# A hybrid DiT on one core: the gated-linear-attention chunk states by one scan per head over a chunk-innermost layout, in place of 38 vector steps

## The chip, the cores and the metric

The kernel runs on one core of one Trainium2 chip. The metric is the device time of one execution in microseconds; what stands below as before's time is the median of three runs.

## The reference

Two layers of a diffusion transformer on 1024 latent and 256 context tokens of width 1024. Layer 0 mixes the tokens with four DeltaNet heads and four gated-linear-attention (GLA) heads, both in two directions; layer 1 is attention; both end in a convolutional feed-forward. What is changed is the GLA heads' recurrence over chunks of 64 tokens:

```python
def _gla_chunked(q, k, v, log_a, s0):
    ...
    b = jnp.cumsum(log_a, axis=3)
    ...
    q_inter = q * jnp.exp(b)
    k_state = k * jnp.exp(b[..., -1:, :] - b)
    a_last = jnp.exp(b[..., -1, :])

    def step(S, xs):
        qd, kd, vc, al = xs
        o = qd @ S
        return S * al[..., :, None] + jnp.swapaxes(kd, -1, -2) @ vc, o

    xs = tuple(jnp.moveaxis(a, 2, 0) for a in (q_inter, k_state, v, a_last))
    S, o_inter = lax.scan(step, s0, xs)
```

There are 20 chunks, 4 of the context and 16 of the latents. The forward direction runs over the context and then the latents, the backward one over each of them from its end. A state is 64 x 128 per direction.

## The kernel before

The kernel is written as one long program; a scheduler then puts each engine's instructions into an order, and each engine runs its list in that order. All DMA transfers are issued from SyncE's queue. The pages below use these names of engines: PE is TensorE, DVE VectorE, ACT ScalarE, POOL GpSimd, SP SyncE.

The stage around the change lies at about 740 to 1040 us. In it four kinds of work are interleaved. `gla_prep(h)` does a GLA head, in the order of heads 0, 1, 3, 2. `gate_t` and `gate_p` project the output gates of all eight heads (tile `pj` on TensorE, 72 matrix products a head, `gt` on ScalarE and VectorE). `dn_run` runs the chunk steps of the last DeltaNet head (`dn_step`: `p`, `r`, `vn`, `sn`, `kd`, `q_`, `o_dn`). `merge` normalises a finished head (`o_g` or `o_d`, `msq`, `mss`, `pmt`) and writes it out for the output projection that follows (`m_scr`, `mt`).

`gla_prep` keeps both directions at once on the partitions: 0 to 63 are the forward one, 64 to 127 the backward one. It goes over the tokens in three groups (`GRP`: 512, 512 and 256). In each the gates' running sum is made by a scan inside the chunks (`g_b`, line 914), from it come the decays, among them `al`, the decay of a whole chunk, one column for each of the 20 chunks. The chunks' products `pgk` (line 953) are copied out of PSUM by ScalarE into `kv` (line 954), which holds 20 blocks of 128 columns. When a head's `kv` is filled, the 2 x 19 steps of the recurrence run on VectorE, each on 64 partitions and 128 columns, and write the state ahead of each chunk into `sst`; line 103 is the helper's line under which the trace shows them. At last the outputs `pgo` are summed in PSUM from the part inside the chunks (line 967, `att` by `v`) and the part from the states (line 970, `qi` by `sst`). One step and one output product read:

```python
            for n in range(19):
                stt(V, sst[0:64, n + 1], sst[0:64, n], al[0:64, n], kv[0:64, n], ALU.mult, ALU.add)
                i, j = SEQB[n], SEQB[n + 1]
                stt(V, sst[64:128, j], sst[64:128, i], al[64:128, i], kv[64:128, i], ALU.mult, ALU.add)
```

Two lines of an earlier stage matter for a price: `kk` turns round a tile inside each partition with ScalarE on partitions 0 to 63, and copies it straight on 64 to 103:

```python
            act(M[0:64], raw_[0:64].rearrange("p j i -> p i j"), AF.Copy, scale=-1.0)
            act(M[64:104], raw_[64:104], AF.Copy, scale=-1.0)
```

Of the kernel before, what the change touches and what calls it, by code (L numbers as in the profile page):

```python
# [9 lines left out]
F32 = mybir.dt.float32  # L10
F32R = mybir.dt.float32r
I32 = mybir.dt.int32
AF = mybir.ActivationFunctionType
ALU = mybir.AluOpType
# [56 lines left out]
def kernel(  # L71
# [4 lines left out]
    ffn_w_up, ffn_conv, ffn_w_down, final_norm, consts, rope, out, dbg=None, stop=None,  # L76
):
    nc = tc.nc
    V, S, G, T = nc.vector, nc.scalar, nc.gpsimd, nc.tensor

    def dma(o, i):
        o = o.bitcast(F32) if o.dtype == F32R else o
        i = i.bitcast(F32) if i.dtype == F32R else i
        nc.sync.dma_start(out=o, in_=i)
# [5 lines left out]
    def act(o, i, f, bias=0.0, scale=1.0):  # L90
        S.activation(out=o, in_=i, func=f, bias=bias, scale=scale)  # L91
# [10 lines left out]
    def stt(e, o, a, s, b, op0, op1):  # L102
        e.scalar_tensor_tensor(out=o, in0=a, scalar=s, in1=b, op0=op0, op1=op1)  # L103

    def pool(stack, name, bufs, psum=False, side=None):
        kw = {"space": PSUM} if psum else {}
        return stack.enter_context(tc.tile_pool(name=name, bufs=bufs, reuse_waits="tile", side=side, **kw))
# [152 lines left out]
    with ExitStack() as p0:  # L260
# [43 lines left out]
        for s_ in range(5):  # L304
            ci = 0 if s_ == 0 else (1 if s_ < 3 else 2)
            o = s_ * 256 - CHUNKS[ci][0]
            d = 1 if ci == 0 else 0
# [12 lines left out]
            t = tmp.tile([128, KD, 256], F32, tag="t", name="t", bufs=2)  # L320
# [47 lines left out]
    def projb(pj, w, sub, ci, n):  # L368
        ps = pj.tile([128, 512], F32, tag="pj", name="pj")
        for k in range(KD):  # L370
            hi, lo = w[k // 4]
            mm3(ps[:, 0:n], hi[:, k % 4, sub * 128:(sub + 1) * 128], lo[:, k % 4, sub * 128:(sub + 1) * 128],
                hhi[ci][:, k], hlo[ci][:, k], k == 0, k == KD - 1)
        return ps
# [100 lines left out]
    with loop:  # L475
# [15 lines left out]
        for ci, (t0, n) in enumerate(CHUNKS):  # L491
            ps = projb(pj, ws, 0, ci, n)
# [347 lines left out]
    with ExitStack() as tl:  # L840
# [4 lines left out]
        gb = pool(ti, "gb", 1)  # L845
# [41 lines left out]
                dma(m_scr[h8, :, t0:t0 + n], gt[:, 0:n])  # L887
            dump(f"m{h8}", m_scr[h8])

        SEQB = [3, 2, 1, 0] + list(range(19, 3, -1))  # L890
        GRP = ((0, 512), (512, 512), (1024, 256))

        def gla_prep(h):
            al = gb.tile([128, 20, 1], F32, tag="al", name="al", bufs=2)
            qi = gb.tile([128, NT], F32, tag="qi", name="qi", bufs=2)
            att = atts[h % 2]
            v = gb.tile([128, NB, 128], F32, tag="gv", name="gv")
            dma(v, gv_scr[h])
            kv = gb.tile([128, 20, 128], F32, tag="kv", name="kv")
            kv2 = kv.rearrange("p (b e) d -> p b e d", e=2)  # L900
            sst = gb.tile([128, 20, 128], F32, tag="sst", name="sst")
            for t0, n in GRP:
                c0, nc_, b0, nb = t0 // 64, n // 64, t0 // 128, n // 128
                ls = gs_.tile([128, 512], F32, tag="ls", name="g_ls", bufs=1)[:, 0:n]
# [2 lines left out]
                b = gs_.tile([128, 512], F32, tag="b", name="g_b")[:, 0:n]  # L907
                eb = gs_.tile([128, 512], F32, tag="eb", name="g_e")[:, 0:n]
                sm_ = gs_.tile([128, 4, 8, 1], F32, tag="gsm", name="gsm")[:, :, 0:nc_]
# [15 lines left out]
                tt(V, sm_[:, 2], sm_[:, 0], sm_[:, 1], ALU.subtract)  # L925
                act(sm_[:, 2], sm_[:, 2], AF.Exp, scale=1.0 / 16)
                act(sm_[:, 3], sm_[:, 1], AF.Exp, scale=1.0 / 16)
                act(al[:, c0:c0 + nc_], sm_[:, 0], AF.Exp, scale=1.0 / 16)
                stt(V, b, q, 0.125, b, ALU.mult, ALU.mult)
                tt(G, eb, k, eb, ALU.mult)  # L930
                tt(V, qi[:, t0:t0 + n].rearrange("p (c t) -> p c t", t=64), b3,
# [3 lines left out]
                for d in range(2):  # L935
                    pa_ = pm.tile([128, 4, 128], F32, tag="pm", name="pga")
                    for i in range(nb):
                        sl = slice(i * 128, (i + 1) * 128)
# [6 lines left out]
                ps = pm.tile([128, 4, 128], F32, tag="pm", name="pgt")  # L945
# [3 lines left out]
                for e in range(2):  # L949
                    ps = pm.tile([128, 4, 128], F32, tag="pm", name="pgk")  # L950
                    pe_ = slice(e * 64, (e + 1) * 64)
                    for i in range(nb):
                        T.matmul(ps[:, i], lhsT=kst[pe_, i], rhs=v[pe_, b0 + i], start=True, stop=True)
                    S.copy(out=kv2[:, b0:b0 + nb, e], in_=ps[:, 0:nb])
            G.memset(sst[0:64, 0], 0.0)
            G.memset(sst[64:128, SEQB[0]], 0.0)
            for n in range(19):
                stt(V, sst[0:64, n + 1], sst[0:64, n], al[0:64, n], kv[0:64, n], ALU.mult, ALU.add)
                i, j = SEQB[n], SEQB[n + 1]
                stt(V, sst[64:128, j], sst[64:128, i], al[64:128, i], kv[64:128, i], ALU.mult, ALU.add)  # L960
            o = gm.tile([128, NB, 128], F32, tag="og", name="o_g", bufs=2)
            for b0 in range(0, NB, 4):
                nb = min(4, NB - b0)
                ps = pm.tile([128, 4, 128], F32, tag="pm", name="pgo")
# [13 lines left out]
        gate_t(0)  # L978
        dn_run(NB)
        o0 = gla_prep(0)  # L980
        o1 = gla_prep(1)
        gate_t(4)
        merge(4, o0)
        gate_t(5)
        merge(1)
        gate_t(6)
        merge(5, o1)
        o3 = gla_prep(3)
        gate_t(2)
        o2 = gla_prep(2)  # L990
# [251 lines left out]
    with ExitStack() as p0:  # L1242
# [4 lines left out]
        with ExitStack() as po:  # L1247
# [32 lines left out]
            for ci in (0, 1, 2):  # L1280
                t0, n = CHUNKS[ci]
                d = 1 if ci == 0 else 0
# [3 lines left out]
                for dt in range(KD):  # L1286
# [3 lines left out]
                    ps = pu.tile([128, 512], F32, tag="u", name="po")  # L1290
# [15 lines left out]
        with ExitStack() as pf:  # L1306
# [7 lines left out]
            step = ffn_ctx(fa, raw, hx)  # L1314
# [13 lines left out]
    with ExitStack() as pf:  # L1328
        p = Ffn()
# [7 lines left out]
    with ExitStack() as pq:  # L1337
# [130 lines left out]
        with ExitStack() as pat:  # L1468
# [8 lines left out]
            scale = 128 ** -0.5  # L1477
# [77 lines left out]
            for i in range(nq + LP + 1):  # L1555
                if i < nq:
                    P_[i] = scores(*its[i // 2], i % 2)
                m = i - LT
                if 0 <= m < nq:
                    T_[m // 2] = transp(P_.pop(m), T_.get(m // 2), m % 2)  # L1560
                m = i - LP
# [8 lines left out]
    with ExitStack() as pe:  # L1570
        ops = ffn_ops(pool(pe, "hE1", 1, side="right"))
        p = Ffn()
# [9 lines left out]
    with ExitStack() as pz:  # L1582
# [4 lines left out]
        for ci in (1, 2):  # L1587
            for b in range(4):
# [3 lines left out]
                for hf in range(2):  # L1592
                    ps = (pu, pd)[(hf if ci == 2 else 0)].tile([128, 512], F32, tag="ud"[(hf if ci == 2 else 0)], name="zt")
# [8 lines left out]
                for hf in range(2):  # L1602
                    sl = slice(hf * 512, (hf + 1) * 512)
# [37 lines left out]
```

## Time and profile before

| | |
|---|---|
| runs | 3491.35, 3484.76, 3500.26 us; median 3491.35 |
| profiled execution, its span | 3491.3 us, 49121 instructions |
| TensorE (PE) busy | 3180.2 us, 91% |
| VectorE (DVE) busy | 2499.8 us, 72% |
| GpSimd (POOL) busy | 1732.5 us, 50% |
| ScalarE (ACT) busy | 1375.7 us, 39% |
| mean granted TensorE clock | 0.954 of full speed |

Busy time is the time in which an engine has an instruction running. It is an average over stages that differ, so what a change in one stage does is read from the stretches of that stage. The granted clock is the share of TensorE's full speed that the chip gave it.

### The profile page before, as it was taken

How to read it: one execution, taken by the hardware profiler on the slowest of the kernel's cores; microseconds unless marked ns; L12 is line 12 of the kernel's file. 1: busy time of each engine (PE TensorE's matmuls, PEld its weight loads, DVE VectorE, ACT ScalarE, POOL GpSimd, SP SyncE). 2: the span in 40 equal slices, each digit the busy share in tenths (PEclk: the TensorE clock that was granted, in tenths of full speed). 3: DMA queues.
4: the chain of work that ended last, by engine and by line, in shares of the span. 5: the costliest groups of instructions: out<-in, count | busy, mean ns of one | idle time of the engine just before them, and what ended most of it. 6: DMA issues, size and time to landing. Idle time of an engine off the chain costs nothing.

```text
span 3491.3 us, 49121 instructions
## 1 busy us (share of the span) xinstructions
PE 3180.2 (91%) x17300; PEld 2678.4 (77%) x17300; DVE 2499.8 (72%) x4119; ACT 1375.7 (39%) x2968; POOL 1732.5 (50%) x1611
## 2 busy tenths in 40 slices
PE   7877988899978988899999998889999799999998
PEld 4766867787767888678888877878888678887877
DVE  5776466668848699776767777887657777767677
ACT  4423133644443455433333323236656433323333
POOL 2364464523335566555555653663333565555554
PEclk9988989999988999999999998999999899999999
DMA  5546455545487444211111211550110111111112
GB/s 187 149 126 167 126 146 146 152 154 171 154 255 213 126 142 136 85 52 58 49 58 48 59 58 60 172 150 28 36 56 29 37 49 43 52 58 49 58 48 74
DMA packets 446165, 350.25 MB, mean 100 GB/s; under 512 B 56756, under 2 KB 392862, under 8 KB 445150
## 3 DMA queue, kind: packets, MB, share of 16 engines
q1 hardware_dynamic: 445918, 347.10, 33.2%
q8 instruction: 137, 2.24, 0.3%
q14 instruction: 110, 0.90, 0.1%
HBM read 286.25 MB, written 60.76 MB: 99 GB/s over the span
## 4 chain that ended last, share of the span: by engine, by line
PE 55%; DVE 21%; DMA 10%; issue 5%; ACT 4%; POOL 4%; SPq 1%; DVEq 0%; ACTq 0%; POOLq 0%
PE fg L157 6%; PE fg L155 6%; PE fg L156 6%; DMA mw<-in_mod_w_dram 4%; PE fd L156 4%; PE fd L157 4%; PE fd L155 4%; DVE macc L103 3%; DVE st L94 2%; DVE ft L103 2%; PE apo L155 2%; PE apo L157 2%; PE apo L156 2%; PE apt L1519 2%; PE pj L155 2%
## 5 line engine op out<-in xcount | busy, mean ns | idle before, releaser
L103 DVE SCALAR_TENSOR_TENSOR xT<-fd,mod,xT 128x512 f32<-128x512 f32 (+1 forms) x480 | 311.0, 671 | 185.3 <-PE fd L157 185.0
L103 DVE SCALAR_TENSOR_TENSOR macc<-mw,sc,macc 128x256 f32<-128x256 f32 (+2 forms) x301 | 241.1, 837 | 73.2 <-DMA mw<-in_mod_w_dram 72.0
L155 PE MATMUL pj<-hhi,whi 128*128 128x512 f32 (+1 forms) x696 | 264.5, 380 | 23.0 <-ACT raw L510 14.8
L156 PE MATMUL fd<-gl,dh 128*128 128x512 f32 (+1 forms) x688 | 267.5, 389 | 7.3 <-DVE gl L94 7.2
L157 PE MATMUL fd<-gh,dl 128*128 128x512 f32 (+1 forms) x688 | 266.7, 388 | 0.0
L155 PE MATMUL fd<-gh,dh 128*128 128x512 f32 (+1 forms) x688 | 262.7, 392 | 1.4 <-ACT gh L1143 1.1
L156 PE MATMUL pj<-hlo,whi 128*128 128x512 f32 (+1 forms) x696 | 262.3, 377 | 0.3 <-DVE hlo L94 0.3
L157 PE MATMUL pj<-hhi,wlo 128*128 128x512 f32 (+1 forms) x696 | 261.7, 376 | 0.0
L94 DVE TENSOR_TENSOR st<-st 128x512 f32<-128x512 f32 x176 | 211.4, 1201 | 47.5 <-POOL s1l L94 34.1
L100 POOL TENSOR_SCALAR P<-P,rc 128x512 f32<-128x512 f32 (+1 forms) x192 | 116.6, 627 | 199.3 <-DVE rc L1505 58.5
L94 POOL TENSOR_TENSOR dl<-sd,dh 128x256 fp32r<-128x256 f32 x168 | 156.4, 946 | 108.6 <-ACT dh L160 108.6
L103 DVE SCALAR_TENSOR_TENSOR ft<-fraw,conv_f,ft 128x1024 f32<-128x1024 f32 (+1 forms) x132 | 169.9, 1287 | 30.1 <-ACT ft L91 29.2
L94 POOL TENSOR_TENSOR w0l<-st,w0h 128x1024 fp32r<-128x1024 f32 x44 | 107.1, 2434 | 145.1 <-ACT w0h L1088 130.6
L155 PEld LDWEIGHTS pj<-hhi,whi 128*128 128x128 f32 x696 | 139.6, 201 | 47.1 <-ACT raw L510 16.3
L94 POOL TENSOR_TENSOR wl<-st,wh 128x512 fp32r<-128x512 f32 x88 | 128.4, 1472 | 83.8 <-ACT wh L160 79.4
L94 POOL TENSOR_TENSOR p<-p,u 128x512 f32<-128x512 f32 (+1 forms) x45 | 94.2, 2093 | 150.6 <-DVE u L94 150.6
L156 PEld LDWEIGHTS fd<-gl,dh 128*128 128x128 f32 x688 | 129.9, 189 | 39.9 <-DVE gl L94 13.5
L155 PEld LDWEIGHTS fd<-gh,dh 128*128 128x128 f32 x688 | 128.1, 189 | 36.6 <-ACT gh L1143 11.3
L156 PEld LDWEIGHTS pj<-hlo,whi 128*128 128x128 f32 x696 | 139.7, 201 | 19.3 <-DVE hlo L94 0.7
L157 PEld LDWEIGHTS pj<-hhi,wlo 128*128 128x128 f32 x696 | 139.2, 200 | 18.8 <-issue 0.2
L157 PEld LDWEIGHTS fd<-gh,dl 128*128 128x128 f32 x688 | 129.9, 189 | 26.3
L156 PE MATMUL fg<-al,w0h 128*128 128x512 f32 (+1 forms) x360 | 141.3, 392 | 6.1 <-DVE al L94 6.1
(623 smaller groups left out, 10466.5 us busy)
## 6 DMA issues: line engine op xcount, KB each, us to landing
st<-in_ffn_w_up_dram SPq DMA_DIRECT2D x88, 512.0 KB
st<-in_ffn_w_up_dram SPq DMA_DIRECT2D x88, 256.0 KB
sd<-in_ffn_w_down_dram SPq DMA_DIRECT2D x176, 128.0 KB
sh<-sh_scr SPq DMA_DIRECT2D x80, 256.0 KB
mw<-in_mod_w_dram SPq DMA_DIRECT2D x128, 128.0 KB
wst<-in_rec_w_in_dram SPq DMA_DIRECT2D x56, 256.0 KB
st<-in_rec_w_out_dram SPq DMA_DIRECT2D x24, 512.0 KB
mw<-in_mod_w_dram SPq DMA_DIRECT2D x24, 512.0 KB
```

What stands on the lines that cost most here:

```text
L94: e.tensor_tensor(out=o, in0=a, in1=b, op=op)
L100: e.tensor_scalar(out=o, in0=a, scalar1=s1, scalar2=s2, op0=op0, op1=op1)
L103: e.scalar_tensor_tensor(out=o, in0=a, scalar=s, in1=b, op0=op0, op1=op1)
L155: T.matmul(ps, lhsT=wh, rhs=xh, start=first, stop=False)
L156: T.matmul(ps, lhsT=wh, rhs=xl, start=False, stop=False)
L157: T.matmul(ps, lhsT=wl, rhs=xh, start=False, stop=last)
L1519: T.transpose(pt_[:, b], P[:, (b0 + b) * 128:(b0 + b + 1) * 128], ident)
```

## The change

The 38 steps become one scan instruction of VectorE over all 128 x 20 columns of a head, both directions at once: in a row of 20 positions the state of a position is the state before it times `d0` plus `kv`. For that `kv` is laid out with the chunks innermost (128 columns of 20 chunks each, so that consecutive state columns of one chunk lie 20 floats, 80 bytes, apart), and shifted by one, with the backward direction turned round: `slots` says which chunk goes to which position. Position 0 is set to zero in `kv` (by GpSimd) and in `al` (by VectorE), so that a row starts anew. `al` is filled by 14 small ScalarE instructions a head in place of 3, `kv` by 14 copies out of PSUM in place of 6. `d0` is `al` repeated for the 128 columns, one ScalarE copy of 128 x 2560; it takes the buffer that `sst` takes after it. The scan works in place on `kv`. Then three ScalarE copies bring the states back into `sst` in the order in which the products read it, two of them backwards. No transfer and no matrix product changes.

```diff
--- before.py
+++ after.py
@@ -887,18 +887,34 @@
                 dma(m_scr[h8, :, t0:t0 + n], gt[:, 0:n])
             dump(f"m{h8}", m_scr[h8])
 
-        SEQB = [3, 2, 1, 0] + list(range(19, 3, -1))
+        def slots(first, n, e, d):
+
+
+            out_ = []
+            for i in range(n):
+                c = 2 * (first + i) + e
+                to = c + 1 if d == 0 else (4 - c if c < 4 else 24 - c)
+                if to == 20:
+                    continue
+                if out_ and out_[-1][0] + out_[-1][1] == i and to == out_[-1][2] + (2 - 4 * d) * out_[-1][1]:
+                    out_[-1][1] += 1
+                else:
+                    out_.append([i, 1, to])
+            step = 2 - 4 * d
+            ends = [t + step * (m - 1) + (1 if step > 0 else -1) for _, m, t in out_]
+            return [(i, m, slice(t, z if z >= 0 else None, step)) for (i, m, t), z in zip(out_, ends)]
+
         GRP = ((0, 512), (512, 512), (1024, 256))
 
         def gla_prep(h):
-            al = gb.tile([128, 20, 1], F32, tag="al", name="al", bufs=2)
+            al = gb.tile([128, 20], F32, tag="al", name="al", bufs=2)
+            V.memset(al[:, 0:1], 0.0)
             qi = gb.tile([128, NT], F32, tag="qi", name="qi", bufs=2)
             att = atts[h % 2]
             v = gb.tile([128, NB, 128], F32, tag="gv", name="gv")
             dma(v, gv_scr[h])
-            kv = gb.tile([128, 20, 128], F32, tag="kv", name="kv")
-            kv2 = kv.rearrange("p (b e) d -> p b e d", e=2)
-            sst = gb.tile([128, 20, 128], F32, tag="sst", name="sst")
+            kv = gb.tile([128, 128, 20], F32, tag="kv", name="kv")
+            G.memset(kv[:, :, 0:1], 0.0)
             for t0, n in GRP:
                 c0, nc_, b0, nb = t0 // 64, n // 64, t0 // 128, n // 128
                 ls = gs_.tile([128, 512], F32, tag="ls", name="g_ls", bufs=1)[:, 0:n]
@@ -925,7 +941,11 @@
                 tt(V, sm_[:, 2], sm_[:, 0], sm_[:, 1], ALU.subtract)
                 act(sm_[:, 2], sm_[:, 2], AF.Exp, scale=1.0 / 16)
                 act(sm_[:, 3], sm_[:, 1], AF.Exp, scale=1.0 / 16)
-                act(al[:, c0:c0 + nc_], sm_[:, 0], AF.Exp, scale=1.0 / 16)
+                for d in range(2):
+                    pd_ = slice(d * 64, (d + 1) * 64)
+                    for e in range(2):
+                        for i, m, sl in slots(b0, nb, e, d):
+                            act(al[pd_, sl], sm_[pd_, 0, 2 * i + e:2 * (i + m - 1) + e + 1:2, 0], AF.Exp, scale=1.0 / 16)
                 stt(V, b, q, 0.125, b, ALU.mult, ALU.mult)
                 tt(G, eb, k, eb, ALU.mult)
                 tt(V, qi[:, t0:t0 + n].rearrange("p (c t) -> p c t", t=64), b3,
@@ -951,13 +971,19 @@
                     pe_ = slice(e * 64, (e + 1) * 64)
                     for i in range(nb):
                         T.matmul(ps[:, i], lhsT=kst[pe_, i], rhs=v[pe_, b0 + i], start=True, stop=True)
-                    S.copy(out=kv2[:, b0:b0 + nb, e], in_=ps[:, 0:nb])
-            G.memset(sst[0:64, 0], 0.0)
-            G.memset(sst[64:128, SEQB[0]], 0.0)
-            for n in range(19):
-                stt(V, sst[0:64, n + 1], sst[0:64, n], al[0:64, n], kv[0:64, n], ALU.mult, ALU.add)
-                i, j = SEQB[n], SEQB[n + 1]
-                stt(V, sst[64:128, j], sst[64:128, i], al[64:128, i], kv[64:128, i], ALU.mult, ALU.add)
+                    for d in range(2):
+                        pd_ = slice(d * 64, (d + 1) * 64)
+                        for i, m, sl in slots(b0, nb, e, d):
+                            S.copy(out=kv[pd_, :, sl].rearrange("p d n -> p n d"), in_=ps[pd_, i:i + m])
+            d0 = gb.tile([128, 128, 20], F32, tag="sst", name="d0")
+            S.copy(out=d0, in_=al[:, None, :].to_broadcast([128, 128, 20]))
+            kvf = kv.rearrange("p d n -> p (d n)")
+            V.tensor_tensor_scan(kvf, d0.rearrange("p d n -> p (d n)"), kvf, 0.0, ALU.mult, ALU.add)
+            sst = gb.tile([128, 20, 128], F32, tag="sst", name="sst")
+            kvn = kv.rearrange("p d n -> p n d")
+            S.copy(out=sst[0:64], in_=kvn[0:64])
+            S.copy(out=sst[64:128, 0:4], in_=kvn[64:128, 3::-1])
+            S.copy(out=sst[64:128, 4:20], in_=kvn[64:128, 19:3:-1])
             o = gm.tile([128, NB, 128], F32, tag="og", name="o_g", bufs=2)
             for b0 in range(0, NB, 4):
                 nb = min(4, NB - b0)
```

What the program's order becomes, at two engines. First TensorE at the last head (head 2), from its last chunk products `pgk` on; the lines with `p` are the DeltaNet head's, `pmt` is another head's merge. Before:

```order
L953 MATMUL pgk<-gv,kst 128x128 x4
L967 MATMUL pgo<-gv,attb_6944 128x128
L970 MATMUL pgo<-sst,qi 64x128 x2
L967 MATMUL pgo<-gv,attb_6944 128x128
L970 MATMUL pgo<-sst,qi 64x128
L421 MATMUL p_7309<-vn,kd 128x128
L422 MATMUL p_7309<-vn,dd 128x128
L408 MATMUL p_7321<-sn,sh 128x128
L409 MATMUL p_7321<-sn,sh 128x128
L970 MATMUL pgo<-sst,qi 64x128
L967 MATMUL pgo<-gv,attb_6944 128x128 x2
```

and after, where the same lines of the code are 973 (`pgk`), 993 and 996 (`pgo`):

```order
L973 MATMUL pgk<-gv,kst 128x128 x4
L993 MATMUL pgo<-gv,attb_6944 128x128
L421 MATMUL p_7356<-vn,kd 128x128
L422 MATMUL p_7356<-vn,dd 128x128
L408 MATMUL p_7369<-sn,sh 128x128
L409 MATMUL p_7369<-sn,sh 128x128
L885 MATMUL pmt<-ident,o_g 128x128 x2
L993 MATMUL pgo<-gv,attb_6944 128x128 x2
L417 MATMUL p_7376<-r,dd 128x128
L996 MATMUL pgo<-sst,qi 64x128 x2
```

The first product that reads `sst` stood second behind `pgk`; seven small products of other kinds and two more of `pgo`'s inner part stand ahead of it now. At the end of head 0 some 60 products stand between, most of them gate projections.

Then ScalarE at the end of head 0 (`q_`, `vn` and `kd` are the DeltaNet head's, `gt` is the eviction of a gate projection, `whi` a part of a weight). Before:

```order
L954 COPY kv<-pgk 128x2x128
L91 ACTIVATE gsm<-gsm 128x8
L954 COPY kv<-pgk 128x2x128
L91 ACTIVATE g_e<-g_b 128x512
L91 ACTIVATE gsm<-gsm 128x8
L91 ACTIVATE g_b<-g_b 128x512
L91 ACTIVATE kd<-sh,ekc 128x128
L160 CAST whi<-wst 128x512
L91 ACTIVATE q__6335<-p_6330,eG 128x128
```

and after (977 fills `kv`, 984 to 986 are the copies into `sst`):

```order
L977 COPY kv<-pgk 64x2x128 x2
L977 COPY kv<-pgk 64x128
L977 COPY kv<-pgk 64x2x128
L91 ACTIVATE q__6335<-p_6330,eG 128x128
L160 CAST whi<-wst 128x512
L91 ACTIVATE gt<-pj 128x512
L419 COPY vn<-p_6337 128x128
L984 COPY sst<-kv 64x2560
L985 COPY sst<-kv 64x512
L986 COPY sst<-kv 64x2048
L91 ACTIVATE kd<-sh,ekc 128x128
```

Two copies have become four, and the three long copies, which need VectorE's scan, stand ahead of the next `kd`, `q_` and `gt` of ScalarE.

## Rows read from the trace of the kernel before

**Rows 1.** The page's part 1: busy us and share of the span.

```profile
PE 3180.2 (91%) x17300; PEld 2678.4 (77%) x17300; DVE 2499.8 (72%) x4119; ACT 1375.7 (39%) x2968; POOL 1732.5 (50%) x1611
```

**Rows 2.** Busy time by 20-us stretches: PE, PEld, DVE, ACT, POOL, clock, DMA share, GB/s.

```profile
780.00:800.00 20.00, 16.74 (x98) 12.54 (x98) 18.70 (x37) 7.38 (x22) 9.42 (x9) 1.00 0.33 95
800.00:820.00 20.00, 18.94 (x132) 15.25 (x132) 12.90 (x31) 11.94 (x58) 5.91 (x8) 1.00 0.58 179
820.00:840.00 20.00, 18.64 (x122) 15.54 (x122) 19.57 (x45) 6.76 (x18) 8.84 (x8) 1.00 0.45 140
840.00:860.00 20.00, 17.67 (x107) 13.50 (x107) 19.11 (x41) 6.13 (x21) 6.80 (x6) 0.91 0.58 189
860.00:880.00 20.00, 19.12 (x138) 16.18 (x137) 10.53 (x24) 11.94 (x55) 8.51 (x9) 1.00 0.68 215
880.00:900.00 20.00, 18.92 (x113) 14.99 (x112) 19.43 (x48) 7.67 (x22) 5.92 (x6) 1.00 0.60 178
900.00:920.00 20.00, 16.20 (x102) 13.24 (x101) 19.25 (x38) 5.59 (x17) 7.33 (x6) 0.83 0.36 113
920.00:940.00 20.00, 20.00 (x124) 15.41 (x122) 14.29 (x36) 11.75 (x57) 7.53 (x7) 1.00 0.57 181
...
980.00:1000.00 20.00, 11.47 (x58) 9.64 (x56) 9.16 (x24) 7.87 (x20) 8.14 (x7) 0.74 0.81 237
1000.00:1020.00 20.00, 10.04 (x46) 8.29 (x46) 4.61 (x11) 9.35 (x30) 9.41 (x5) 0.59 0.94 299
```

**Rows 3.** The same for `sst` alone: PE, PEld, DVE, POOL, clock, DMA share.

```profile
780.00:800.00 20.00, 2.18 (x16) 0.97 (x16) 10.76 (x18) 0.00 (x0) 1.00 0.33 95
...
820.00:840.00 20.00, 0.00 (x0) 0.00 (x0) 6.75 (x15) 0.00 (x0) 1.00 0.45 140
840.00:860.00 20.00, 3.78 (x24) 1.65 (x24) 9.99 (x23) 0.00 (x0) 0.91 0.58 189
...
880.00:900.00 20.00, 0.00 (x0) 0.00 (x0) 6.66 (x15) 0.00 (x0) 1.00 0.60 178
900.00:920.00 20.00, 1.76 (x16) 0.79 (x16) 10.20 (x18) 0.00 (x0) 0.83 0.36 113
```

**Rows 4.** Groups by line and form, 740 to 1030 us: count, busy, mean ns, idle.

```profile
L103 DVE SCALAR_TENSOR_TENSOR sst<-sst,al,kv 64x128 f32<-64x128 f32 x152 | 67.7, 445 | 7.0 <-ACT kv L954 3.3 <-POOL wlo L94 0.2
...
L954 ACT COPY kv<-pgk 128x512 f32<-128x512 f32 x16 | 9.0, 582 | 3.4 <-PE pgk L953 3.3
...
L914 DVE TENSOR_TENSOR_SCAN g_b<-reset,g_ls 128x512 f32<-128x512 f32 x6 | 7.2, 1203 | 0.0
...
L914 DVE TENSOR_TENSOR_SCAN g_b<-reset,g_ls 128x256 f32<-128x256 f32 x4 | 2.7, 679 | 0.0
L954 ACT COPY kv<-pgk 128x256 f32<-128x256 f32 x8 | 2.7, 376 | 1.3 <-PE pgk L953 1.3
```

**Rows 5.** ScalarE's groups by line and form over the whole span.

```profile
L91 ACT ACTIVATE M<-pp 64x1024 f32<-64x1024 f32 x4 | 8.2, 2058 | 14.8 <-DMA pp<-nd_scr 14.8
...
L91 ACT ACTIVATE rm_sq<-xT 128x2048 f32<-128x2048 f32 x4 | 7.5, 1911 | 7.5 <-DVE xT L103 7.5
...
L91 ACT ACTIVATE M<-pp 40x1024 f32<-40x1024 f32 x4 | 4.2, 1054 | 0.1
```

**Rows 6.** TensorE's timeline in gate projections: start, us, what.

```profile
812.60 0.40 PE L156 MATMUL pj<-hlo,whi 128*128 128x512 f32 x1
812.83 0.40 PE L157 MATMUL pj<-hhi,wlo 128*128 128x512 f32 x1
813.07 0.38 PE L421 MATMUL p<-vn,kd 128*128 128x128 f32 x2
813.29 0.39 PE L422 MATMUL p<-vn,dd 128*128 128x128 f32 x2
```

**Rows 7.** TensorE's timeline after the last head: first and fifth DeltaNet round.

```profile
976.54 0.38 PE L421 MATMUL p<-vn,kd 128*128 128x128 f32 x2
...
990.99 0.49 PE L421 MATMUL p<-vn,kd 128*128 128x128 f32 x2 [0.41 <-ACT vn L419]
```

## The prediction

> **What bounds the kernel now.** I began with the page's table of engines [rows 1]: TensorE is busy for 91% of the span, VectorE for 72%, ScalarE for 39%. Over the whole program TensorE is the bound, so the change can only gain where TensorE waits. The second view is therefore the table by 20-us stretches over the stage in which the recurrence runs [rows 2]. There VectorE alternates: in five stretches (780, 820, 840, 880 and 900) it is busy for 18.7 to 19.6 of 20 us, and in those TensorE is busy for 16.20 to 18.92 only, at a granted clock down to 0.91 and 0.83. In the three stretches between them in which a head ends (800, 860, 920) VectorE falls to 10.5–14.3, while ScalarE rises from about 6–7 to 11.8–11.9. From 980 to 1020 TensorE is down to 11.47 and 10.04, with the DMA engines 81% and 94% busy: that is the tail of the stage, not bound by VectorE.
>
> The third view takes the same stretches for the state tile `sst` alone [rows 3]: VectorE's 18 + 15 + 23 + 15 + 18 recurrence steps take 44.36 us of its 96.06 in the five saturated stretches. In the grouped lines [rows 4] all 152 steps cost 67.7 us, 445 ns each. So the operation that the change takes off VectorE is what saturates it there.
>
> **A. What VectorE's relief gives back.** In the five stretches TensorE is idle for 100 − 88.17 = 11.8 us, and its clock is short by 20 × 0.09 + 20 × 0.17 = 5.2 us' worth [rows 2]. VectorE would have at most 96.06 − 44.36 + 4 × 5.4 = 73.3 us to do there in place of 96.06 (5.4 is the scan, below), so it would no longer bind. The most it can give is 11.8 + 5.2 = 17.0 us; I take **−17**, which is generous, and half of it, −8.5, as the other end. TensorE's 17 us are all that this stage can give back: a gain above 0.5% (17.5 us; about what a measurement of this kernel can tell from no change) would need all of it and nothing lost.
>
> **B. The new serial wait at each head's end.** Before, a step needs only its own chunk's product, so most of the 38 steps run while later products are still made, and the first output product `pgo<-sst` can run once its chunk's state is there. After, nothing can start before the last chunk product of the head is in `kv`, and then come three things in a row, on three engines.
>
> The last group's copies of `kv` out of PSUM: four in the new order, split by direction, where two of 376 ns stood [rows 4]; a copy's time goes by its elements per partition, so 4 × 376 = 1.5 us.
> The scan over 2560 elements of a partition. The scans that the kernel has take 1203 ns for 512 and 679 for 256 [rows 4], 2.05 ns an element, so 679 + 2304 × 2.05 = 5.4 us. Its inputs lie in a row, as theirs do.
> The three ScalarE copies of 2560, 512 and 2048 elements that turn `kv` back into `sst`; they read with a stride of 80 bytes. The nearest strided read is `M<-pp` in `kk` (a 32x32 transpose inside each partition), which reads at 128 bytes over 64 partitions: 2058 ns for 1024 elements, against 1054 for the one behind it, over the other 40 partitions, that reads straight [rows 5]. Taking off some 0.17 us an instruction (what is left of 582 and 376 at 0.80 ns an element [rows 4]), that is 1.84 ns an element: 5120 × 1.84 + 3 × 0.17 = 9.9 us. At the straight price (1911 for 2048 [rows 5], 0.84 ns an element) it is 4.8. I take 9.9, because the only row with such a stride says so; that two copies also run backwards no row prices, and I give it nothing.
> With some 0.6 us for three hand-offs the wait is 1.5 + 5.4 + 9.9 + 0.6 = **17.4 us** (12.3 at the straight price).
>
> The Trainium skill, "Advanced Engine Details and Errata", section "SBUF Cachelines", says that SBUF works in lines of 16 bytes and that an access pattern needs at least two hits on a line to hide the access time. The trace agrees for reads, 2058 against 1054 ns [rows 5], and by that rule the copies would be dear, as I take them. It makes no exception for writes; what that would do is the third rival.
>
> What hides this wait is what TensorE has between the last `pgk` and the first `pgo<-sst` in its new order. For head 0 that is 27 projections of 512 columns, 24 of 256 and 9 small ones; the starts of 512-column ones lie 0.23 us apart, those of small ones 0.22 (two passes each) [rows 6], and 256 columns get half of 0.23, so 6.2 + 2.9 + 2.0 = 11.1 us. Heads 1 and 3 have 12.4 and 11.7 in the same way (27 + 24 + 15, 28 + 24 + 11). The last head, 2, has 7 small products: 1.5 us. TensorE so stands for 17.4 − 11.1 = 6.3, then 5.0, 5.7 and 15.9 us: **+32.9**. At the straight price it stands for 1.2, 0, 0.6 and 10.8: +12.6.
>
> **C. ScalarE fuller, and others queued behind it.** ScalarE runs in order. The broadcast copy `d0` (2560 elements, straight: 2.3 us) and the three copies add 12.2 us a head. The stretches after a head's end have 11.9 us of ScalarE's time taken already [rows 2]: 24.1 of 20, 4.1 too much, 12.3 for the three. Its neighbours (6.8, 6.1, 7.7, 5.6) can take part of it. While the copies run, the evictions of the gate projections (`gt<-pj`), the DeltaNet's `vn`, `kd` and `q_` stand behind them. I take a third, **+4**, between 0 and 12.3. The small copies of `al` (14 for 3), the two memsets and VectorE's `al` column cost nothing in the sum: they stand among the work of the earlier groups, where ScalarE and GpSimd are busy for less than half of most stretches [rows 2]. If uncovered, the last group's four of `al`, each below the 376 ns of a 256-column copy, would add up to 1.5 us a head.
>
> **D. The tail.** The DeltaNet rounds left over after the last head end the stage: after the last `pgo` before has seven, the first at 976.54 and the fifth at 990.99, 3.6 us apart [rows 7]. In the new order five stand behind the last `pgo<-sst`, two within the wait. So 2 × 3.6 = **−7.2**.
>
> Sum: −17 + 32.9 + 4 − 7.2 = +12.7. The profiled execution's span is 3491.3, the median of the runs 3491.35, so nothing has to be added: **3504 us**.
>
> **The rivals.**
> *Strided reads at the straight price.* For it: an 80-byte stride is less than the row's 128. Against it: both rows are of the same engine and line, and both patterns touch each 4 bytes far from the last. B is 12.6: −17 + 12.6 + 4 − 7.2 = −7.6, **3484**.
> *ScalarE becomes the bound* (the other side). The new `kv` copies write at 80 bytes; no row has ScalarE writing with a stride. If a write costs as a strided read does, 11.7 us of `kv` copies in the stage [rows 4] become about 23, 2.9 more a head, of which some 1 us is in the last group's, on the path: 4 us. The stretch after a head is then 27.0 of 20 in place of 24.1, 3 × 2.9 = 8.7 more that the neighbours no longer take. +12.7 + 4 + 8.7 = +25.4: **3517**. It decides where ScalarE is over some 17 of 20 us in two stretches running. For it: a projection's eviction is one of those that queue, and TensorE has just so many PSUM buffers to write. Against: ScalarE is at 39% over all. The skill's rule quoted above speaks for it.
> *The last head's wait is hidden by the tail.* From 980 the DMA engines are 81 and 94% busy [rows 2], and what ends the stage may be transfers that go on during the wait. Then the last 15.9 and D fall away: −17 + 17.0 + 4 = +4, **3495**. Against it: the DeltaNet rounds wait for ScalarE's `vn`, not for a transfer, and `vn` stands behind the copies.
>
> **How the numbers follow.** The forecast, 3504 (its own range 3495 to 3514), has 0.40: 0.28 of it within 0.5% (3474 to 3509), 0.12 slower. Strided reads straight: 0.22 (0.05 faster, 0.17 same): faster needs the last head hidden too (B 1.8), C at nothing, and TensorE's idle time at 800 and 860 back as well (1.06 + 0.88 [rows 2]), −17 + 1.8 − 1.9 = −17.1. ScalarE the bound: 0.24 (0.22 slower, 0.02 same). Hidden last head: 0.14 (0.03 faster, 0.11 same). Together 0.08 faster, 0.58 same, 0.34 slower. The range goes from that −17.1, 3474, to the upper ends of the terms, −8.5 + 32.9 + 4 + 12.3 − 7.2 = +33.5: 3525.
>
> **What the new profile would show.** The scan at 5.4 us and the copies at 4.9, 1.1 and 3.9 (straight: 2.3, 0.6, 1.9); the last-group `kv` copies at 0.2 to 0.4 each, or twice that (third rival). VectorE below 16 of 20 in every stretch of 780 to 960. TensorE idle before `pgo<-sst` for some 5 to 6 us with ScalarE's `sst` copies as releaser, thrice, and about 16 us before the last head's. If these waits are under 2 us, the forecast is too high; if TensorE waits for `gt<-pj` instead, too low. It would also be wrong if the relief on VectorE gave TensorE nothing, since its waits in those stretches were for something else.

## The result and the profile after

The changed kernel took 3536.84 us in the median (3534.07 to 3550.45) against 3488.06 us for the kernel before in the same comparison: ratio 1.0139, 95% interval 1.0118 to 1.016, so slower by some 48 us. The forecast was 3504 with a range up to 3525. The profiled execution has a span of 3532.5 us, 41.2 more than before's.

The page's first part, after; beside [rows 1] ScalarE has 94 us more and VectorE 29 less:

```profile
PE 3193.1 (90%) x17300; PEld 2689.1 (76%) x17300; DVE 2470.7 (70%) x3975; ACT 1469.5 (42%) x3060; POOL 1743.6 (49%) x1607
```

The groups of lines by form in the stage (740 to 1080 us): count, then busy us and mean ns, then the idle time before. They answer to [rows 4, 5]:

```profile
L977 ACT COPY kv<-pgk 64x512 f32<-64x512 f32 x24 | 29.2, 1215 | 1.2 <-PE pgk L973 1.0
L984 ACT COPY sst<-kv 64x2560 f32<-64x2560 f32 x4 | 22.1, 5524 | 17.0 <-DVE kv L981 17.0
L981 DVE TENSOR_TENSOR_SCAN kv<-d,kv 128x2560 f32<-128x2560 f32 x4 | 22.0, 5512 | 4.4 <-ACT kv L977 4.4
...
L986 ACT COPY sst<-kv 64x2048 f32<-64x2048 f32 x4 | 17.8, 4446 | 0.0
...
L977 ACT COPY kv<-pgk 64x256 f32<-64x256 f32 x24 | 15.7, 694 | 0.8 <-PE pgk L973 0.6
...
L979 ACT COPY d<-al 128x2560 f32<-128x2560 f32 x4 | 9.3, 2330 | 0.1
...
L985 ACT COPY sst<-kv 64x512 f32<-64x512 f32 x4 | 5.0, 1251 | 0.0
...
L977 ACT COPY kv<-pgk 64x128 f32<-64x128 f32 x8 | 3.6, 450 | 0.1
```

The scan and `d0` cost what was forecast (5.4 and 2.3 us). The copies into `sst` cost 11.2 us a head in place of 9.9. The `kv` copies cost 48.5 us in place of before's 11.7: a 512-element one takes 1215 ns where it took 582, and there are 56 in place of 24.

The table by 20-us stretches, after (columns as in [rows 2]):

```profile
780.00:800.00 20.00, 18.17 (x116) 15.27 (x116) 14.58 (x21) 14.39 (x30) 12.42 (x8) 1.00 0.41 125
800.00:820.00 20.00, 16.76 (x88) 12.10 (x89) 3.54 (x9) 15.73 (x22) 3.69 (x5) 0.83 0.30 92
820.00:840.00 20.00, 19.64 (x134) 16.95 (x135) 16.70 (x34) 17.87 (x58) 11.39 (x9) 1.00 0.50 158
...
860.00:880.00 20.00, 13.72 (x74) 10.81 (x72) 9.24 (x10) 15.76 (x16) 8.86 (x4) 0.91 0.56 172
...
900.00:920.00 20.00, 18.84 (x133) 16.06 (x132) 17.69 (x36) 16.41 (x35) 9.36 (x8) 1.00 0.62 196
...
940.00:960.00 20.00, 17.27 (x111) 12.68 (x110) 6.08 (x16) 16.32 (x55) 4.76 (x4) 0.91 0.22 71
...
980.00:1000.00 20.00, 6.88 (x50) 5.13 (x48) 10.45 (x16) 14.64 (x18) 1.34 (x2) 0.76 0.76 235
```

No stretch has VectorE saturated any more; the two highest, 16.70 and 17.69 of 20 us, are a little above the 16 that the forecast named. What is new are the stretches at a head's end, 800, 860, 940 and 980: VectorE is down to 3.5 to 10.5 us, TensorE to 6.9 to 17.3, its clock to 0.76 to 0.91, while ScalarE, with the long copies, is at 14.6 to 16.3.

The timeline of the last head shows the wait itself (start, length, engine, line):

```profile
983.74 0.72 PE L973 MATMUL pgk<-gv,kst 64*128 64x128 f32 x8 [0.56 <-ACT kst L968]
...
984.48 2.51 ACT L977 COPY kv<-pgk 64x256 f32<-64x256 f32 x4 [0.63 <-PE pgk L973]
...
987.02 5.49 DVE L981 TENSOR_TENSOR_SCAN kv<-d,kv 128x2560 f32<-128x2560 f32 x1 [1.12 <-ACT kv L977]
...
992.61 5.52 ACT L984 COPY sst<-kv 64x2560 f32<-64x2560 f32 x1 [4.58 <-DVE kv L981]
992.82 0.79 PE L417 MATMUL p<-r,dd 128*128 128x128 f32 x2 [5.26 <-DVE r L103]
998.14 1.25 ACT L985 COPY sst<-kv 64x512 f32<-64x512 f32 x1
999.30 4.45 ACT L986 COPY sst<-kv 64x2048 f32<-64x2048 f32 x1
...
999.45 0.70 PE L996 MATMUL pgo<-sst,qi 128*64 128x128 f32 x4 [5.84 <-ACT sst L985]
```

From 984.48 to 1003.75 the three engines work one after the other, 19.3 us (forecast 17.4). TensorE stops twice, 5.26 us for the DeltaNet's `r`, which stands behind the scan on VectorE, and 5.84 for the states.

What TensorE waits for, grouped by its line and the releaser, 740 to 985 us: total, times, longest:

```profile
PE pj L155 <- DVE gt L103: 9.0, 3, 3.4
PE pgo L996 <- ACT sst L986: 6.3, 3, 2.7
```

The first line is in no list of before's waits: at the ends of three heads the gate projections stop for some 3 us each, since `gt`, which frees their PSUM buffer, stands behind the scan.

Where the 41 us lie, from the first and last starts of groups: the first `pgk` starts 1.9 us later (764.8, 766.7), the last `pgo<-sst` 37.8 later (974.7, 1012.5); the first `xtr` of the next stage 31.2 later (1003.5, 1034.7), so 6.6 come back in the DeltaNet's tail; the last product of the output projection 41.1 later (1170.7, 1211.8). From there on both run alike. Of the 1.9 nothing can be said: the first `pgk` starts between 760.6 and 768.6 in the runs below.

### The profile page after: what moved, and what is told of

Read it like the earlier page. It is cut to its first block, busy times and chain, and to the rows that moved or that the text cites. A ratio compares the mean times of both kernels' runs of the same rounds, so it can differ in the third digit from the quotient of the medians.

```text
span 3532.5 us, 49048 instructions
## 1 busy us (share of the span) xinstructions
PE 3193.1 (90%) x17300; PEld 2689.1 (76%) x17300; DVE 2470.7 (70%) x3975; ACT 1469.5 (42%) x3060; POOL 1743.6 (49%) x1607
## 3 DMA queue, kind: packets, MB, share of 16 engines
q1 hardware_dynamic: 445918, 347.10, 32.9%
## 4 chain that ended last, share of the span: by engine, by line
PE 55%; DVE 19%; DMA 9%; issue 6%; ACT 5%; POOL 4%; SPq 1%; DVEq 0%; ACTq 0%; POOLq 0%
PE fg L157 6%; PE fg L155 6%; PE fg L156 6%; DMA mw<-in_mod_w_dram 5%; PE fd L156 4%; PE fd L157 4%; PE fd L155 4%; DVE macc L103 3%; DVE st L94 2%; PE apo L155 2%; PE apo L157 2%; PE apo L156 2%; DVE ft L103 2%; PE apt L1545 2%; PE pj L155 2%
## 5 line engine op out<-in xcount | busy, mean ns | idle before, releaser
L103 DVE SCALAR_TENSOR_TENSOR ft<-fraw,conv_f,ft 128x1024 f32<-128x1024 f32 (+1 forms) x132 | 169.7, 1286 | 31.2 <-ACT ft L91 30.3
L156 PEld LDWEIGHTS fd<-gl,dh 128*128 128x128 f32 x688 | 129.8, 189 | 38.6 <-DVE gl L94 12.1
L155 PEld LDWEIGHTS fd<-gh,dh 128*128 128x128 f32 x688 | 128.2, 188 | 35.7 <-ACT gh L1169 10.2
L156 PEld LDWEIGHTS pj<-hlo,whi 128*128 128x128 f32 x696 | 140.0, 201 | 19.5 <-DVE hlo L94 0.7
L157 PEld LDWEIGHTS pj<-hhi,wlo 128*128 128x128 f32 x696 | 139.4, 200 | 19.3
L155 PE MATMUL fg<-ah,w0h 128*128 128x512 f32 (+1 forms) x360 | 140.6, 391 | 6.2 <-ACT ah L1058 6.2
```

What stands on the lines that cost most here:

```text
L155: T.matmul(ps, lhsT=wh, rhs=xh, start=first, stop=False)
L156: T.matmul(ps, lhsT=wh, rhs=xl, start=False, stop=False)
L157: T.matmul(ps, lhsT=wl, rhs=xh, start=False, stop=last)
```

## The experiments

Theory **load**: ScalarE's time as such sets the stage (`kv` 48.5, `sst` 44.9, `d0` 9.3 us, where before had 11.7). Theory **wait**: what counts is the chain from the last chunk product to the outputs. Ratios are to the kernel before in the same comparison; 0.1% is 3.5 us.

### The copies into sst read straight

```diff
-            kvn = kv.rearrange("p d n -> p n d")
+            kvn = kvf.rearrange("p (n d) -> p n d", d=128)
```

> The changed kernel with the three copies into sst reading kv in a straight row (the values they carry are not those of the chunks they stand for). Every engine's order is that of the changed kernel. Its trace has 5524, 1251 and 4446 ns for the three; straight they should take about 2330 (as d0), 0.6 and 1900, so 4 x 6.4 = 26 us less ScalarE time and 6.4 us less wait at each head's end. Theory load (ScalarE's own time in the stage sets it: 48.5 us of kv copies where before had 11.7, 44.9 of sst copies, 9.3 of d0): about half comes back, 3520 to 3528. Theory wait (scan and copies in a row at each head's end, with TensorE, gt and vn queued behind): the wait falls from about 20 to 13 us a head, 3508 to 3518.

Ratio 1.0094 (1.0077 to 1.011), 3517.05 us. The three copies took 2333, 616 and 1894 ns. So 25.5 us less of copies, all in the wait, gave back 0.45%, some 16 us. Both theories allow it, wait rather.

### The kv copies write straight

```diff
-            G.memset(kv[:, :, 0:1], 0.0)
+            kvw = kv.rearrange("p d n -> p (d n)").rearrange("p (n d) -> p n d", d=128); G.memset(kvw[:, 0], 0.0)
...
-                            S.copy(out=kv[pd_, :, sl].rearrange("p d n -> p n d"), in_=ps[pd_, i:i + m])
+                            S.copy(out=kvw[pd_, sl], in_=ps[pd_, i:i + m])
```

> The changed kernel with the 14 kv copies a head writing rows of 128 floats in place of single floats 80 bytes apart (they so land in other places than the scan takes them for). Every engine's order is that of the changed kernel. Copies of 64x512 should fall from 1215 to about 580 ns, 64x256 from 694 to 375, so 48.5 to about 25 us of ScalarE, of which only some 1.2 us a head lie in the wait behind the last chunk product. Theory load: 3512 to 3522. Theory wait: 3530 to 3536, about 5 us back.

Ratio 1.0122 (1.0106 to 1.0137), 3527.86 us: 24 us less of `kv` copies gave back some 6 us by the ratio, and the intervals overlap. The time lies in neither range; 6 us back is near what theory wait named (5) and short of what load asked for.

### Both straight

The two edits above at once.

> Both edits at once, same order on every engine; ScalarE keeps the 14 copies and d0, all straight. Theory load: nearly all comes back, 3485 to 3500. Theory wait: the scan (5.5 us), the straight copies (4.8) and the queue behind the scan stay, 3502 to 3515.

Ratio 1.0056 (1.0041 to 1.0071), 3503.81 us. Together the strides cost 0.83%, some 29 us; 0.56%, some 20 us, stay with every copy straight. Every engine's order is that of the changed kernel, so these 29 us are the strides' alone.

### The kernel before with ScalarE's load

```diff
-                    S.copy(out=kv2[:, b0:b0 + nb, e], in_=ps[:, 0:nb])
+                    for d in (0, 1, 0, 1):
+                        pd_ = slice(d * 64, (d + 1) * 64)
+                        S.copy(out=kv2[pd_, b0:b0 + nb, e], in_=ps[pd_, 0:nb])
```

> The kernel before with only ScalarE's load of kv copies added: each copy split by direction and made twice, straight, so four times 11.7 = about 47 us of kv copies in place of 11.7. The 38 vector steps and their chunk-by-chunk waits stay; the scheduler's order moves somewhat. Theory load: slower by 15 to 35 us, 3503 to 3523. Theory wait: within 6 us of before.

Ratio 1.0046 (1.0026 to 1.0065), 3500.19 us, with 47.3 us of `kv` copies. By its ratio, some 16 us slower, this is a hit for load. But each of these copies also stands between a product and the steps that wait for it (VectorE's steps were idle for 12.1 us behind `kv`, before 3.3 [rows 4]), so it does not tell time from time in a chain. The extra copies below do.

### Both straight, without the scan

```diff
-            V.tensor_tensor_scan(kvf, d0.rearrange("p d n -> p (d n)"), kvf, 0.0, ALU.mult, ALU.add)
```

> The straight copies of both kinds as before, and the scan left out, so that the copies into sst wait for the last kv copy alone and nothing on VectorE stands behind 5.5 us (the recurrence is not computed; the scheduler's order moves where the scan stood). ScalarE's load is that of the kernel with both kinds straight. Theory load: no more than 5 us below it, 3499 to 3504. Theory wait: the remaining loss against before is the scan and the queue behind it, so 3480 to 3492.

Ratio 0.9978 (0.9966 to 0.999), 3483.86 us: 0.78% below the kernel with the scan, some 27 us for 22.8 us of scan, with the same work for ScalarE. Load fails here. The scheduler's order is another one, with 36 products of TensorE in place of 69 between the first head's last `pgk` and its first `pgo<-sst`; what that does to the 27 us is not shown.

### Both straight, kv copies undivided

```diff
-                    for d in range(2):
-                        pd_ = slice(d * 64, (d + 1) * 64)
-                        for i, m, sl in slots(b0, nb, e, d):
-                            S.copy(out=kvw[pd_, sl], in_=ps[pd_, i:i + m])
+                    kve = kvw.rearrange("p (b e) d -> p b e d", e=2)
+                    S.copy(out=kve[:, b0:b0 + nb, e], in_=ps[:, 0:nb])
```

> Both kinds straight, and the kv copies again six a head over all 128 partitions, as before had them (the backward half so lands where the scan does not expect it): kv copies 11.7 us in place of 24.3. Theory load: 5 to 10 us come back, 3494 to 3499. Theory wait: up to 0.8 us a head of the wait, 3500 to 3505.

Ratio 1.0046 (1.0029 to 1.0063), 3506.31 us: within the interval of both straight (1.0056). The difference is some 3 us, with an uncertainty of some 8, so this run tells neither theory from the other; it shows no clear price of the division into 14 copies once they are straight.

### Both straight, the scan off the path

```diff
-            V.tensor_tensor_scan(kvf, d0.rearrange("p d n -> p (d n)"), kvf, 0.0, ALU.mult, ALU.add)
+            so = gb.tile([128, 1024], F32, tag="so", name="so")
+            for c, z in ((0, 1024), (1024, 2048), (2048, 2560)):
+                V.tensor_tensor_scan(so[:, 0:z - c], kvf[:, c:z], kvf[:, c:z], 0.0, ALU.min, ALU.add)
```

> Both kinds of copies straight, and the scan kept at its place on VectorE with its 2560 elements a head (three pieces in a row, since only 4 KB are free), but it writes to a tile that nothing reads: the copies into sst wait for kv alone, while gt, sn and r still stand behind the scan on VectorE. Theory serial wait (the outputs wait for copies, scan and copies in a row): as without the scan, 3480 to 3490. Theory queue (what stands behind the scan on VectorE keeps TensorE): as with it, 3498 to 3506. Half each, 3490 to 3497.

Ratio 0.9977 (0.9961 to 0.9992), 3484.48 us: as without a scan, with the same order of TensorE's products, though VectorE spends 24.1 us in all on the scans behind the four heads' last `kv` copies. Its timeline at the end of the second head:

```profile
846.79 2.33 ACT L986 COPY sst<-kv 64x2560 f32<-64x2560 f32 x1
848.43 6.12 DVE L983 TENSOR_TENSOR_SCAN so<-kv 128x1024 f32<-128x1024 f32 x3
...
849.14 1.91 ACT L988 COPY sst<-kv 64x2048 f32<-64x2048 f32 x1
...
851.47 0.44 PE L998 MATMUL pgo<-sst,qi 128*64 128x128 f32 x4
...
854.47 0.66 DVE L103 SCALAR_TENSOR_TENSOR gt<-gt,pj 128x512 f32<-128x512 f32 x1
```

The states are there before the scan ends, the outputs run beside it, and `gt` still stands behind it. A third theory, that the scan costs because VectorE's queue stands behind it, falls as it was put: that queue costs nothing as long as TensorE has the outputs to do.

### Both straight, d0 copied three times

```diff
-            S.copy(out=d0, in_=al[:, None, :].to_broadcast([128, 128, 20]))
+            for _ in range(3): S.copy(out=d0, in_=al[:, None, :].to_broadcast([128, 128, 20]))
```

> Both kinds straight, and d0 copied three times in place of once: 18.6 us more of ScalarE in the stage, ahead of the last kv copies and so out of the wait. If ScalarE's time as such is dear (the strided reads' 25 us cost some 16), 10 to 14 us above the kernel with both kinds straight, 3512 to 3518; if only time inside the wait is dear, within 5 us of it, 3500 to 3508.

Ratio 1.0049 (1.0028 to 1.007), 3507.32 us, no more than the 1.0056 without them. The trace has the 18.6 us:

```profile
L979 ACT COPY d<-al 128x2560 f32<-128x2560 f32 x12 | 27.9, 2326 | 0.2
```

ScalarE's time outside the wait costs nothing measurable here.

### The changed kernel, copies shared with other engines

```diff
-                            S.copy(out=kv[pd_, :, sl].rearrange("p d n -> p n d"), in_=ps[pd_, i:i + m])
+                            (S.copy, V.tensor_copy)[d](out=kv[pd_, :, sl].rearrange("p d n -> p n d"), in_=ps[pd_, i:i + m])
...
-            S.copy(out=sst[64:128, 0:4], in_=kvn[64:128, 3::-1])
-            S.copy(out=sst[64:128, 4:20], in_=kvn[64:128, 19:3:-1])
+            V.tensor_copy(out=sst[64:128, 0:4], in_=kvn[64:128, 3::-1])
+            V.tensor_copy(out=sst[64:128, 4:20], in_=kvn[64:128, 19:3:-1])
```

> The changed kernel with the backward half's kv copies and sst copies made by VectorE, which has about 35 of 60 us in use in this stage; what it computes is the reference. ScalarE loses some 24 and 23 us, VectorE gets them; the two halves of the copies into sst run side by side, so the wait falls by 5.7 us a head. Both theories: 3508 to 3520; if strided accesses cost VectorE less than ScalarE, the lower end. If VectorE's longer queue is the next limit, above 3520.

Ratio 1.0112 (1.0094 to 1.0131), 3530.44 us: 0.27% back, less than both theories gave and within the two intervals; a time above 3520 was expected for the case that VectorE's longer queue is the next limit, which is not shown. In the other form GpSimd has the backward copies, beside ScalarE's, and the scan is cut in four:

```diff
-            V.tensor_tensor_scan(kvf, d0.rearrange("p d n -> p (d n)"), kvf, 0.0, ALU.mult, ALU.add)
+            for c in range(0, 2560, 640):
+                V.tensor_tensor_scan(kvf[:, c:c + 640], d0f[:, c:c + 640], kvf[:, c:c + 640], 0.0, ALU.mult, ALU.add)
...
-            S.copy(out=sst[0:64], in_=kvn[0:64])
-            S.copy(out=sst[64:128, 0:4], in_=kvn[64:128, 3::-1])
-            S.copy(out=sst[64:128, 4:20], in_=kvn[64:128, 19:3:-1])
+            G.tensor_copy(out=sst[64:128, 0:4], in_=kvn[64:128, 3::-1])
+            S.copy(out=sst[0:64, 0:4], in_=kvn[0:64, 0:4])
+            S.copy(out=sst[0:64, 4:20], in_=kvn[0:64, 4:20])
+            G.tensor_copy(out=sst[64:128, 4:20], in_=kvn[64:128, 19:3:-1])
```

> The changed kernel, computing the reference, with the backward half's copies into sst made by GpSimd beside ScalarE's forward ones, these in two (4 and 16 chunks), and the scan in four pieces. The wait's last part falls from 11.2 us to the longer of the two engines. If GpSimd's strided read is no dearer than ScalarE's (4.5 us for 2048 elements): 5.5 us a head less, 3515 to 3525. If it costs twice as much, no change, 3530 to 3540.

Ratio 1.0114 (1.009 to 1.0139), 3530.81 us, another miss. The copies did run side by side, at the same price on both engines, but the scan's pieces took 28.5 us in all in place of 22.0:

```profile
L982 DVE TENSOR_TENSOR_SCAN kv<-d,kv 128x640 f32<-128x640 f32 x16 | 28.5, 1837 | 3.5 <-ACT kv L977 3.4
L987 ACT COPY sst<-kv 64x2048 f32<-64x2048 f32 x4 | 17.8, 4450 | 0.0
L988 POOL COPY sst<-kv 64x2048 f32<-64x2048 f32 x4 | 17.8, 4443 | 0.0
```

1.6 us a head of the 5.5 taken out of the wait went into the scan. Why the rest did not come back in these two is not shown.

### Paired steps: no scan, chunks outermost

```diff
+            for n in range(19):
+                stt(V, kv[:, n + 1], kv[:, n], al[:, n + 1:n + 2], kv[:, n + 1], ALU.mult, ALU.add)
+            G.tensor_copy(out=sst[64:128, 0:4], in_=kv[64:128, 3::-1])
+            for c in (0, 8, 16):
+                S.copy(out=sst[0:64, c:min(20, c + 8)], in_=kv[0:64, c:min(20, c + 8)])
+            G.tensor_copy(out=sst[64:128, 12:20], in_=kv[64:128, 11:3:-1])
+            G.tensor_copy(out=sst[64:128, 4:12], in_=kv[64:128, 19:11:-1])
```

These lines stand in place of `d0`, the scan and the three copies. `kv` is here `[128, 20, 128]`, filled in the order of `slots`, so one step serves both directions.

> A third form that computes the reference: kv with the chunks outermost again but in the order of the recurrence for each direction, so that 19 steps of 128x128 serve both directions at once in place of 38 of 64x128; no scan and no d0; straight copies of the states into sst, forward ones by ScalarE, backward ones by GpSimd. VectorE has 19 x 4 x 0.36 = 27 us in place of 67.7, ScalarE 12.6 more for kv and 9.3 for sst. Theory wait: the steps follow the chunks again, only the last copies are added at a head's end, 3482 to 3494. Theory load: 3490 to 3500.

Ratio 0.9984 (0.9972 to 0.9996), 3485.4 us, the only form that computes the reference and is not behind the kernel before. Its gain is some 6 us, within the 0.5% called no change, though its interval ends below 1. Its steps took 36.7 us, where 27 were expected.

```profile
L103 DVE SCALAR_TENSOR_TENSOR kv<-kv,al 128x128 f32<-128x128 f32 x76 | 36.7, 483 | 2.7 <-ACT kv L977 1.0
L977 ACT COPY kv<-pgk 64x512 f32<-64x512 f32 x24 | 13.9, 578 | 1.8 <-PE pgk L973 1.6
```

## Why the prediction was wrong

The sign was that of the forecast; its size was not, 12.7 us against some 48. The profiled executions, one of each, differ by 41.2 us, and what follows takes these apart. The stage, from the first `pgk` to the end of the last `pgo<-sst`, in before, after, scan off the path and both straight (columns as in [rows 2]):

```profile
764.80:974.90 210.10, 196.33 (x1270) 157.94 (x1269) 170.21 (x386) 85.23 (x312) 67.67 (x61) 0.98 0.50 155
...
766.70:1012.80 246.10, 209.58 (x1296) 169.00 (x1296) 139.90 (x253) 183.09 (x409) 82.10 (x62) 0.91 0.49 152
...
768.60:961.00 192.40, 191.67 (x1267) 154.53 (x1266) 138.13 (x249) 129.67 (x392) 68.55 (x57) 1.00 0.56 174
...
763.40:982.80 219.40, 199.87 (x1296) 162.74 (x1295) 139.70 (x253) 135.37 (x409) 82.45 (x62) 0.95 0.55 171
```

What a stretch has beyond TensorE's busy time is time in which TensorE stands: 13.8, 36.5, 0.7 and 19.5 us. From before to after the stage is 36.0 us longer, 22.7 of it standing and 13.3 TensorE's products; the tail gives 6.6 back, 10 lie behind the stage, and the first `pgk` is 1.9 later.

**A, VectorE's relief, −17.** Within the stage it came out. The run with the scan off the path has all of the change but the serial scan and the strides; TensorE stands there for 13.0 us less than before (11.8 forecast), and its products take 4.7 us less, at a clock of 1.00 in place of 0.98 (5.2 forecast). The whole program kept only −0.23%, some −8 us, the other end that A named: the tail is 3.9 us longer, the time behind the stage 2.4, and the first `pgk` 3.8 later.

**B, the wait, +32.9.** As time in which TensorE stands, it came out, by errors that cancel. Between a head's last `pgk` and the end of its last `pgo<-sst` after has 5.1, 6.9, 5.3 and 13.4 us of it, 30.6 in all; over the stage TensorE stands for 35.8 us more than with the scan off the path. The wait was longer than B's: 19.3 us at the last head in place of 17.4, since the copies read at 2.1 ns an element and not 1.84, and the last `kv` copies took 2.5 us and not 1.5. With 19.3 at every head B's covers would leave 40.5, so other work hid more than B allowed, in part because it ran more slowly (below). The gate projections did run in the wait, 51 or 52 a head at the first three heads, as B counted. But what TensorE stood for there was not the first state: it was `gt` behind the scan (9.0 us in three pieces), which B didn't have and the prediction named as a sign of too low a forecast, and ScalarE's last copy (6.3 us in three), behind which only the later outputs wait.

**The step that failed: what such a wait costs.** The sum took the wait as standing alone. It priced all other products at the spacing of full clock, 0.22 and 0.23 us, and of the clock it had only A's gain. In after the clock over the stage is 0.91, lower than the 0.98 of before. Eight pieces of the stage, 44.3 us together, are at 0.50 (1.2 of 2.4 GHz), and each of them begins while TensorE stands or up to 1.6 us after it stood. TensorE works for 34.8 us in these pieces; before has 10.2 us at 0.50 and 8.6 of work in them. The same small products start 0.43 us apart in such a piece and 0.22 outside:

```profile
978.78 0.63 PE L421 MATMUL p<-vn,kd 128*128 128x128 f32 x2
979.21 0.64 PE L422 MATMUL p<-vn,dd 128*128 128x128 f32 x2
...
984.71 0.39 PE L421 MATMUL p<-vn,kd 128*128 128x128 f32 x2
984.93 0.39 PE L422 MATMUL p<-vn,dd 128*128 128x128 f32 x2
```

If half of the work at 0.50 is what the low clock costs, an estimate from these starts, after loses some 13 us to it more than before, where the sum had a gain of 5.2: 18 of the 28.5 us between the 12.7 and the 41.2. Both straight and after have the same products in the same order, and the copies' strides alone between them: 17.0 us more of standing and 9.7 us more for the same products. Against before, work adds to it: 26 products more stand ahead of the last `pgo<-sst`, 19 of them DeltaNet products, which before had in its tail. How the low clock and this work divide the 13.3 us is not shown.

By the ratios the two halves of the wait cost 1.62%, some 56 us from the scan off the path to the changed kernel, 27 with the scan and 29 with the strides, each uncertain by some 8 or 9 us; the profiled executions give 17.8 and 30.8. The strides' part stands on equal orders. The scan's does not, and some 7.5 us of it lie behind the stage (below).

**C, ScalarE fuller, +4.** It measured about nothing: 18.6 us more of ScalarE outside the wait changed no time. What it said of the queue behind the copies belongs to B.

**D, the tail, −7.2.** It measured −6.6 (28.8 us from the last `pgo<-sst` to the first `xtr` before, 22.3 after). The products of the rounds that left the tail run in the stage instead, where the sum gave them no time.

**A term that was not in the sum.** From the first `xtr` to the end of the output projection the profiles have 167.2 us before and 177.1 after: 10 us behind the stage. Both straight has the same order there and the same 177.1, the two with one kind straight 176.8 and 181.5; paired steps, in another order, 168.4, the scan off the path 169.6. So it seems to go with the order in which the scheduler puts this projection and its weight transfers, seen in one profiled execution each. A late transfer alone is not it: the first `mw` is issued 26.5 us after the first `xtr` before and 31.8 after, but 30.5 in paired steps. TensorE's wait for `macc`, which is made from `mw`, grew from 1.6 to 7.7 us; the scan off the path has 6.6 of it too. The cause stays open. It is part of what the ratios above give to the scan wherever a run's order differs.

**The rivals.** Strided reads at the straight price: wrong, 5524 against 2333 ns. The last head's wait hidden: wrong, its last output came 37.8 us late where the head before it was 27.0 late. ScalarE as the bound: its price for the writes was right (1215 against 577 ns), and its 3517 was nearest, but by another mechanism, since ScalarE's time alone costs nothing. Its figure of 23 us for `kv` was also short: the copies are split by direction, and each half takes as long as the whole did, so 24.3 us straight and 48.5 strided. The Trainium skill, "Advanced Engine Details and Errata", section "SBUF Cachelines", makes no exception for writes, and these runs agree: 1215 ns at 80 bytes against 577 in a row.

## What to carry to other kernels

A recurrence in small steps that follow their inputs is partly done when its last input comes; one long instruction over all of them begins only then, and its whole length, with the copies into and out of its layout, lies between the last product and the first output. Count other work as cover only as far as its own evictions don't stand in a queue behind a link of that chain. And price more than the standing: in this kernel the clock fell to half after TensorE had stood, and the products that ran then took longer. When the small steps are too many, make each one wider, as the paired steps do, which cost nothing here, before making one instruction of them.

## What the runs showed of the hardware

ScalarE's copy out of PSUM into single floats 80 bytes apart took 1215 ns for 512 elements, against 577 into a row; VectorE's took 1226. Reads of SBUF at 80 bytes cost ScalarE 4446 ns for 2048 elements and GpSimd 4443, straight 1892 for ScalarE; VectorE took 2282:

```profile
L977 DVE COPY kv<-pgk 64x512 f32<-64x512 f32 x8 | 9.6, 1226 | 7.2 <-ACT kv L977 7.1
...
L986 DVE COPY sst<-kv 64x2048 f32<-64x2048 f32 x4 | 9.1, 2282 | 0.0
```

These two lines are of the form that shares the copies with VectorE. A copy over 64 partitions takes as long as one over 128 (577 and 582 ns for 512 elements), so on one engine splitting by partitions doubles the time.
